# A two-layer hybrid transformer on one core: two-operand GpSimd work of the mixers on VectorE, the softmax's multiplication by 1/l on ScalarE

## The chip, the cores and the metric

The kernel runs on one core of a Trainium2 chip. A core has TensorE (PE: matmuls and transposes; PEld is its loading of stationary operands), VectorE (DVE), ScalarE (ACT), GpSimd (POOL) and SyncE (SP, which here issues DMAs). Each engine works through its own list of instructions in order; semaphores hold an instruction until what it needs is there. The metric is the device time of one execution in microseconds (us); the median of three runs is used.

## The reference

512 tokens of width 1024 pass two layers, each a mixer and a convolutional feed-forward part, all in float32.

```python
for i in range(DEPTH):                      # DEPTH = 2
    h = rmsnorm(x, mix_norms[i])
    x = x + (even_mixer(h, positions, *mixers[0]) if i % 2 == 0 else odd_mixer(h, *mixers[1]))
    x = x + conv_ffn(rmsnorm(x, ffn_norms[i]), *ffns[i])
return rmsnorm(x, final_norm)
```

The even mixer has two kinds of softmax attention. Twelve MLA heads attend causally over all keys; their queries and keys come from low-rank projections. Four heads (DSW) attend in three dilated windows at once, with rotary positions on query and key, and the three windows are merged by their sums. Both use `p = exp(s - max)`, `l = sum(p)`, `(p / l) @ v`.

The odd mixer has a state-space part (SSD) in 4 chunks of 128 tokens with 16 heads of 64, and 8 heads of stick-breaking attention:

```python
xdt = x * dt                                # SSD, per head and chunk
y_diag = (C B^T * decay) @ xdt
state = state * chunk_decay + B^T (xdt * decay_end)
y = y_diag + exp(cs) * (C @ state_before) + x * d_skip
log_w = log_sigmoid(z) + (sum of log_sigmoid(-z) over later keys)   # stick-breaking
y = exp(log_w) @ v
```

## The kernel before, in words

Activations lie transposed: 128 features on partitions, 512 tokens along the free dimension. To keep float32 accuracy, each operand of a matmul is split in a high part (a copy rounded to fp32r, mostly by ScalarE) and a low part (the rest, mostly by VectorE), and a product is three matmuls. So each tile that TensorE is to read costs ScalarE one pass and VectorE one pass. Weights come in chunks of up to 1024 columns by DMA (`wraw`), and `wchunk` (line 213) splits them: `whi` on ScalarE (line 219), `wlo` (line 221) on the engine named by `self.lo`: VectorE in the mixers, GpSimd in the two feed-forward parts. The change does not touch that.

Within a mixer, projections are cut in pieces of three to six matmuls and filled between the heads' own steps (`Stream.fill`); numbers written out by hand set how many. TensorE's order is fixed in that way (`InOrder`). For the other engines a scheduler sets the order of a queue when the program is built, from the dependences and its estimates.

Even mixer (line 644). `sincos` makes `cos` and `sin`; line 704 multiplies both by the token norms. For each of 12 query and key tiles of DSW, `run_qk` (line 719) evicts the projection twice: ScalarE writes `raw` (729), VectorE writes `rot = proj * cos` (730). Four DMAs of SP swap the 32-row quarters of `raw` into `sw` (733). Then `sw *= sin` (734) and `rot += sw` (735). `run_mla` makes the MLA operands: `vt` (759), `knp` (764), `rt` (773) and its split `qk` (264 and 265), and the key's halves `kh`, `kl` (871, 872).

`softmax` (line 572) works on one block of 128 queries, 64 times in all (16 heads of 4 blocks): VectorE adds the mask and takes the maximum (578), scales it (580); ScalarE takes the exponential and its sum `l` (581, two instructions: ACTIVATE and the read of the accumulator); VectorE takes the reciprocal (582); line 583 multiplies the block by it. Then TensorE transposes the probabilities, ScalarE and VectorE evict them as `pth` (600, 951) and `ptl` (601, 952), and TensorE multiplies with the values. While one head does this, the scores of the next are made. Two PSUM banks hold scores, two the transposes, two the results, two the projections.

Odd mixer, SSD (line 1118). `prepare` (1285) makes, for each half of the heads and each chunk, `xd = x * dt` (1292), its split `xdt` (1296, 1297), `xs *= d` (1300), `xd *= decay_end` (1302) and its split `xe` (264, 265). `states` (1307) makes the running state `stt`: the old one times the decay (1318), plus the new (1320), and its split `ph`. `past` (1323) adds the contribution of the state: `yof` (1332), `xs += yof` (1334). `weights` makes the decayed `C B^T` of a head (`sg`, 1348 and 1351) and its split `mh`; `apply` multiplies it with `xdt` and adds to `xs` (1366).

Stick-breaking attention (line 1441 on, heads from line 1497). A head has three banks. Each goes through ScalarE (1528 to 1530), VectorE (`ab`, 1531), a triangular select on GpSimd (1510), the split `sh` (a cast, 1535) and `sl` (1536), sums on TensorE, an exponential (1555), the select again, the split `wh` (a cast, 1559) and `wl` (1560), and the product with the values.

Of the kernel before, what the change touches and what calls it, by code (L numbers as in the profile page):

```python
# [10 lines left out]
F32 = mybir.dt.float32  # L11
# [3 lines left out]
AF = mybir.ActivationFunctionType  # L15
ALU = mybir.AluOpType
PSUM = bass.MemoryType.PSUM

P = 128
# [164 lines left out]
class Builder:  # L184
# [387 lines left out]
    def softmax(self, pool, s, n, tag, bufs, scale, mask):  # L572

        nc = self.nc
        st = pool.tile([P, 4], F32, tag="st", name=self.nm("st"), bufs=5)
        mx, nmx, l, rl = (st[:, k : k + 1] for k in range(4))
        t = pool.tile([P, n], F32, tag=tag, name=self.nm(tag), bufs=bufs)
        nc.vector.tensor_tensor_reduce(out=t, in0=s[:, :n], in1=mask, scale=1.0, scalar=-3.0e38,  # L578
                                       op0=ALU.add, op1=ALU.max, accum_out=mx)
        nc.vector.tensor_scalar(nmx, mx, -scale, None, op0=ALU.mult)  # L580
        nc.scalar.activation(t, t, AF.Exp, bias=nmx, scale=scale, accum_out=l)
        nc.vector.reciprocal(rl, l)  # L582
        nc.gpsimd.tensor_scalar(t, t, rl, None, op0=ALU.mult)  # L583
        return t

    def pv_steps(self, pool, o, blocks, v, first, last):
# [57 lines left out]
    def even_mixer(self, pool):  # L644
        nc, a = self.nc, self.a
# [55 lines left out]
        (qlh, qll), (klh, kll) = ([[t[k] for t in lh[c]] for k in range(2)] for c in (slice(0, 2), slice(2, 3)))  # L701

        for t in (cr, sr):
            nc.gpsimd.tensor_tensor(t, t, r, op=ALU.mult)

        masks = pool.tile([P, N_MASK], BF16, tag="masks", name="masks")
        for c0 in range(0, N_MASK, T):
# [11 lines left out]
        def run_qk(p, g, s):  # L719
            def run(w):  # L720
                for ps in self.proj_pieces(w, xh, xl):
                    yield
                raw = pool.tile([P, T], F32, tag="fr", name=self.nm("raw"), bufs=2)
                sw = pool.tile([P, T], F32, tag="fr", name=self.nm("sw"), bufs=2)
                t = pool.tile([P, T], F32, name=self.nm("rot"), tag="raw", bufs=8)
                view = k_order if s and g else q_order
                if s and not g:
                    view = lambda t, ordered=True: t
                nc.scalar.activation(raw, ps, AF.Copy)
                nc.vector.tensor_tensor(view(t), view(ps, False), view(cr, False), op=ALU.mult)  # L730
                for b in range(4):
                    o_ = b ^ 1
                    nc.sync.dma_start(sw[b * 32 : b * 32 + 32], raw[o_ * 32 : o_ * 32 + 32])
                nc.gpsimd.tensor_tensor(sw, sw, sr, op=ALU.mult)
                nc.gpsimd.tensor_tensor(view(t), view(t), view(sw, False), op=ALU.add)
                raws[p, g, s] = t

            return f"d{p}{g}{s}", lambda: self.wchunk(a["wqk0"][(p * 3 + g) * 2 + s], D), run
# [379 lines left out]
    def ssd(self, pool, sub, xh, xl, xs, ZS, zs, others):  # L1118
# [166 lines left out]
        def prepare(g):  # L1285

            xds = []
            for c in range(NB):
                x8 = xs[g][:, c].rearrange("p (h d) -> p h d", h=8)
                tq = lambda k: tok[:, k, c, g * 8 : g * 8 + 8, None].to_broadcast([P, 8, 64])  # L1290
                xd = sub.tile([P, 8, 64], F32, tag="xd", name=self.nm("xd"), bufs=2)
                (nc.vector if c % 2 else nc.gpsimd).tensor_tensor(xd, x8, tq(0), op=ALU.mult)
                for q in range(2):
                    h4 = slice(4 * q, 4 * q + 4)
                    sp = sub.tile([P, 4, 2, 64], F32R, name=self.nm("xdt"), **XD)
                    nc.scalar.activation(sp[:, :, 0, :], xd[:, h4], AF.Copy)
                    nc.vector.tensor_tensor(sp[:, :, 1, :], xd[:, h4], sp[:, :, 0, :].bitcast(F32), op=ALU.subtract)
                    xdt[g, c, q] = sp

                nc.gpsimd.tensor_tensor(x8, x8, dbc[:, g * 8 : g * 8 + 8, None].to_broadcast([P, 8, 64]), op=ALU.mult)  # L1300
                if c < NB - 1:
                    nc.gpsimd.tensor_tensor(xd, xd, tq(3), op=ALU.mult)
                    xde[g, c] = self.split(xd.rearrange("p h d -> p (h d)"), sub, "xe", bufs=6)

        state = {}
# [1 line left out]
        def states(g, c):  # L1307
# [6 lines left out]
            if c == 0:  # L1314
                nc.vector.tensor_copy(cur, ps)
            else:
                dec = cdec[:, c, g * 8 : g * 8 + 8, None].to_broadcast([P, 8, 64])
                nc.gpsimd.tensor_tensor(cur.rearrange("p (h d) -> p h d", h=8),
                                        state[g, c - 1][0].rearrange("p (h d) -> p h d", h=8), dec, op=ALU.mult)
                nc.vector.tensor_tensor(cur, ps, cur, op=ALU.add)  # L1320
            state[g, c] = cur, self.split(cur, sub, "ph", bufs=2)

        def past(g, c):
# [7 lines left out]
            tt = sub.tile([P, T], F32, tag="sg", name=self.nm("yof"), bufs=4)  # L1331
            nc.vector.tensor_tensor(tt.rearrange("p (h d) -> p h d", h=8),
                                    po.rearrange("p (h d) -> p h d", h=8), ec, op=ALU.mult)
            nc.gpsimd.tensor_tensor(xs[g][:, c], xs[g][:, c], tt, op=ALU.add)

        mix = {}

# [103 lines left out]
    def stick(self, pool, sub, zs, y, qkvs, others):  # L1441
# [55 lines left out]
        def head(h):  # L1497
# [41 lines left out]
            def sums(bi):  # L1539
# [17 lines left out]
                wh = sub.tile([P, T], F32R, tag="wh", name=self.nm("wh"), bufs=2)  # L1557
                wl = sub.tile([P, T], F32R, tag="wl", name=self.nm("wl"), bufs=2)
                nc.vector.tensor_copy(wh[:, :w], ab[:, :w])
                nc.gpsimd.tensor_tensor(wl[:, :w], ab[:, :w], wh[:, :w].bitcast(F32), op=ALU.subtract)  # L1560
                hd.w[bi] = wh, wl

            def apply(bi):
# [134 lines left out]
```

## Time and profile before

| | |
|---|---|
| median of 3 runs | 1465.1 us (1463.52 to 1468.44) |
| the profiled execution | 1463.86 us, its span 1462.1 us |
| instructions | 18180 |
| mean granted TensorE clock | 0.985 of full speed |
| DMA | 121.22 MB, mean 83 GB/s |

The span runs from the first to the last instruction. In the span, 0 to 338 us is the even mixer with its norms and first projections, 338 to 703 us the first feed-forward part, 703 to 1097 us the odd mixer (its SSD heads from about 772 to 910 us, its stick-breaking heads from about 910 to 1045 us), and the rest the second feed-forward part. Busy time is what an engine spent in instructions; a row that names a wait gives how long an engine stood idle before an instruction and what ended that. Granted clock is what a throttle gave TensorE; it is 1.00 or 0.50 at a time, and a mean over a stretch lies between.

### The profile page before, as it was taken

Reading aid. Unit: us, or ns where it says so; the run is one execution under the profiler, and the core shown is the slowest. Engines: PE = TensorE matmul, PEld = TensorE weight load, DVE = VectorE, ACT = ScalarE, POOL = GpSimd, SP = SyncE. Lnnn points to the kernel's source line nnn. Section 1 sums busy time; section 2 is a strip of 40 time slices with the busy share of each in tenths; the row PEclk is TensorE's granted clock in tenths of the full one; section 3 lists DMA queues with packets and bytes.
Section 4 is the critical chain, followed back from the end, with each engine's and each line's share of the span. In section 5 each row is a group of like instructions: output and inputs, shape, how many; then the busy total and the mean of one; then the engine's idle time right before and its main releaser. Section 6 shows DMA issues by size and latency. Waiting matters only on the chain.

```text
span 1462.1 us, 18180 instructions
## 1 busy us (share of the span) xinstructions
PE 1388.7 (95%) x6796; PEld 1146.8 (78%) x6796; DVE 863.6 (59%) x1362; ACT 663.2 (45%) x1085; POOL 597.1 (41%) x391
## 2 busy tenths in 40 slices
PE   7899899899999999999988898998999999999997
PEld 5777687687888888888877677787888888888886
DVE  7878678746555555122668987678555555552124
ACT  5557457535433333222446465777344333333222
POOL 2454445303655555444102420434215555554441
PEclk9999999999999999999999999999999999999998
DMA  4421212122322322333222111111233233223333
GB/s 166 120 62 55 69 55 69 39 81 73 101 93 95 101 101 85 105 92 95 92 72 73 44 44 58 46 58 40 62 101 101 87 102 101 91 97 94 100 98 98
DMA packets 40264, 121.22 MB, mean 83 GB/s; under 512 B 5232, under 2 KB 8304, under 8 KB 40176
## 3 DMA queue, kind: packets, MB, share of 16 engines
q1 hardware_dynamic: 38160, 117.92, 25.4%
q10 hardware_dynamic: 2016, 2.14, 0.5%
q8 instruction: 54, 0.88, 0.3%
q14 instruction: 34, 0.28, 0.1%
HBM read 114.80 MB, written 2.10 MB: 80 GB/s over the span
## 4 chain that ended last, share of the span: by engine, by line
PE 80%; DVE 12%; ACT 4%; issue 3%; POOL 1%; DMA 1%; DVEq 0%; SPq 0%; ACTq 0%; POOLq 0%
PE proj L113 50%; PE o L113 19%; PE z L113 5%; PE s L113 3%; PE t L116 2%; DVE wlo L221 2%; PE t L113 1%; ACT whi L219 1%; DVE mh L265 1%; DVE sg L1351 0%; DVE cv L1150 0%; DVE xs L1366 0%; DVE xl L331 0%; DVE s L578 0%; DVE rot L730 0%
## 5 line engine op out<-in xcount | busy, mean ns | idle before, releaser
L221 POOL TENSOR_TENSOR wlo<-wraw,whi 128x1024 fp32r<-128x1024 f32 (+1 forms) x135 | 315.2, 2336 | 323.7 <-ACT whi L219 323.7
L219 ACT ACTIVATE whi<-wraw 128x1024 fp32r<-128x1024 f32 (+3 forms) x219 | 222.2, 1015 | 365.0 <-PE proj L113 328.7
L113 PE MATMUL proj<-xh,whi 128*128 128x512 f32 x844 | 343.0, 406 | 8.8 <-ACT xh L330 6.7
L113 PE MATMUL proj<-xh,wlo 128*128 128x512 f32 x844 | 334.1, 396 | 1.4 <-DVE wlo L387 1.1
L113 PE MATMUL proj<-xl,whi 128*128 128x512 f32 x844 | 333.9, 396 | 1.2 <-DVE xl L331 1.2
L113 PE MATMUL proj<-act,whi 128*128 128x512 f32 (+1 forms) x748 | 219.3, 377 | 0.0
L113 PEld LDWEIGHTS proj<-xh,whi 128*128 128x128 f32 x844 | 161.3, 191 | 41.0 <-ACT xh L330 8.7
L113 PEld LDWEIGHTS proj<-xh,wlo 128*128 128x128 f32 x844 | 160.9, 191 | 37.6 <-DVE wlo L387 1.5
L113 PEld LDWEIGHTS proj<-xl,whi 128*128 128x128 f32 x844 | 161.2, 191 | 31.3 <-DVE xl L331 3.1
L113 PEld LDWEIGHTS proj<-act,whi 128*128 128x128 f32 x748 | 137.7, 188 | 25.8
L113 PE MATMUL o<-xh,wlo 128*128 128x512 f32 x368 | 143.4, 390 | 0.0
L113 PE MATMUL o<-xh,whi 128*128 128x512 f32 x368 | 143.3, 389 | 0.0
L113 PE MATMUL o<-xl,whi 128*128 128x512 f32 x368 | 143.2, 389 | 0.0
L113 PE MATMUL proj<-act,wlo 128*128 128x512 f32 (+1 forms) x374 | 140.8, 376 | 0.0
L583 POOL TENSOR_SCALAR s<-s,st 128x512 f32<-128x512 f32 (+1 forms) x64 | 81.2, 1274 | 109.4 <-DVE st L582 82.3
L366 DVE TENSOR_TENSOR x<-x,proj 128x512 f32<-128x512 f32 x31 | 21.2, 684 | 171.0 <-PE proj L113 170.9
L221 DVE TENSOR_TENSOR wlo<-wraw,whi 128x1024 fp32r<-128x1024 f32 (+3 forms) x84 | 100.0, 1190 | 27.3 <-ACT whi L219 26.3
L524 DVE SCALAR_TENSOR_TENSOR cv<-gt,cols,cv 128x511 f32<-128x511 f32 x44 | 94.3, 2148 | 35.9 <-ACT cv L523 35.9
L528 POOL TENSOR_TENSOR sl<-sl,rsr 128x512 f32<-128x512 f32 x44 | 57.8, 1313 | 94.3 <-ACT sl L527 94.3
L527 ACT ACTIVATE sl<-cv 128x512 f32<-128x512 f32 x44 | 27.8, 631 | 127.3 <-DVE cv L525 127.3
L533 DVE TENSOR_TENSOR up<-sl,o 128x512 f32<-128x512 f32 x44 | 30.3, 688 | 91.8 <-POOL sl L528 91.8
L265 DVE TENSOR_TENSOR act<-up,act 128x512 fp32r<-128x512 f32 x44 | 63.3, 1438 | 29.3 <-ACT act L264 29.3
(305 smaller groups left out, 2250.9 us busy)
## 6 DMA issues: line engine op xcount, KB each, us to landing
wraw<-in_g SPq DMA_DIRECT2D x44, 512.0 KB, 3.3
wraw<-in_u SPq DMA_DIRECT2D x44, 512.0 KB, 3.3
wraw<-in_d SPq DMA_DIRECT2D x32, 448.0 KB, 3.3
wraw<-in_wqk SPq DMA_DIRECT2D x20, 512.0 KB, 3.5
wraw<-in_d SPq DMA_DIRECT2D x17, 512.0 KB, 3.5
wraw<-in_wx SPq DMA_DIRECT2D x12, 512.0 KB, 3.4
wraw<-in_wv SPq DMA_DIRECT2D x10, 512.0 KB, 3.6
wraw<-in_wz SPq DMA_DIRECT2D x8, 512.0 KB, 3.3
```

The source lines that it names most:

```text
L113: return self._put(self.b.nc.tensor.matmul(*args, **kw))
L116: return self._put(self.b.nc.tensor.transpose(*args))
L219: nc.scalar.activation(hi[:, :n], raw[:, :n], AF.Copy)
L221: (eng or self.lo).tensor_tensor(lo[:, :n], raw[:, :n], hi[:, :n].bitcast(F32), op=ALU.subtract)
L265: nc.vector.tensor_tensor(lo, src, hi.bitcast(F32), op=ALU.subtract)
L366: self.nc.vector.tensor_tensor(self.x[m], self.x[m], ps, op=ALU.add)
L524: nc.vector.scalar_tensor_tensor(c[:, 1:], gt[:, : T - 1], col_(1), c[:, 1:], op0=ALU.mult, op1=ALU.add)
L527: nc.scalar.activation(s, c, AF.Silu)
L528: nc.gpsimd.tensor_tensor(s, s, r, op=ALU.mult)
L533: nc.vector.tensor_tensor(u, s, pu, op=ALU.mult)
L583: nc.gpsimd.tensor_scalar(t, t, rl, None, op0=ALU.mult)
```

## The change

Lines keep their numbers. Line 583, the multiplication of a probability block by 1/l, becomes a copy with a per-partition scale on ScalarE. Lines 704, 734, 735, 1292 (its half that was on GpSimd), 1300, 1302, 1318, 1334 and 1560 go from GpSimd to VectorE with the same operands. GpSimd keeps the selects of line 1510, the conversions of the masks, four squares at the start (654), and its work in the feed-forward parts and the end.

```diff
@@ softmax
         nc.vector.reciprocal(rl, l)
-        nc.gpsimd.tensor_scalar(t, t, rl, None, op0=ALU.mult)
+        nc.scalar.activation(t, t, AF.Copy, scale=rl)
@@ even_mixer
         for t in (cr, sr):
-            nc.gpsimd.tensor_tensor(t, t, r, op=ALU.mult)
+            nc.vector.tensor_tensor(t, t, r, op=ALU.mult)
...
-                nc.gpsimd.tensor_tensor(sw, sw, sr, op=ALU.mult)
-                nc.gpsimd.tensor_tensor(view(t), view(t), view(sw, False), op=ALU.add)
+                nc.vector.tensor_tensor(sw, sw, sr, op=ALU.mult)
+                nc.vector.tensor_tensor(view(t), view(t), view(sw, False), op=ALU.add)
@@ ssd, prepare
-                (nc.vector if c % 2 else nc.gpsimd).tensor_tensor(xd, x8, tq(0), op=ALU.mult)
+                nc.vector.tensor_tensor(xd, x8, tq(0), op=ALU.mult)
...
-                nc.gpsimd.tensor_tensor(x8, x8, dbc[:, g * 8 : g * 8 + 8, None].to_broadcast([P, 8, 64]), op=ALU.mult)
+                nc.vector.tensor_tensor(x8, x8, dbc[:, g * 8 : g * 8 + 8, None].to_broadcast([P, 8, 64]), op=ALU.mult)
                 if c < NB - 1:
-                    nc.gpsimd.tensor_tensor(xd, xd, tq(3), op=ALU.mult)
+                    nc.vector.tensor_tensor(xd, xd, tq(3), op=ALU.mult)
@@ ssd, states and past
-                nc.gpsimd.tensor_tensor(cur.rearrange("p (h d) -> p h d", h=8),
+                nc.vector.tensor_tensor(cur.rearrange("p (h d) -> p h d", h=8),
...
-            nc.gpsimd.tensor_tensor(xs[g][:, c], xs[g][:, c], tt, op=ALU.add)
+            nc.vector.tensor_tensor(xs[g][:, c], xs[g][:, c], tt, op=ALU.add)
@@ stick, sums
-                nc.gpsimd.tensor_tensor(wl[:, :w], ab[:, :w], wh[:, :w].bitcast(F32), op=ALU.subtract)
+                nc.vector.tensor_tensor(wl[:, :w], ab[:, :w], wh[:, :w].bitcast(F32), op=ALU.subtract)
```

The order of TensorE's and SP's instructions stays as it was. VectorE's and ScalarE's queues change at many places; three follow. Tiles carry the program's names with a number for the buffer.

ScalarE at the first softmax of the even mixer (in the profile before at 69 to 78 us), first before:

```order
L581 ACT_TABLE_LOAD
L581 ACTIVATE s_127_657,st_656<-s_127_657,st_656 128x512
L581 ACTIVATE s_130_671,st_670<-s_130_671,st_670 128x384
L581 ACTIVATE s_133_685,st_684<-s_133_685,st_684 128x256
L581 ACTIVATE s_136_699,st_698<-s_136_699,st_698 128x128
L219 ACTIVATE whi_746<-wraw_744 128x1024
```

The same place of ScalarE's queue now:

```order
L581 ACT_TABLE_LOAD
L581 ACTIVATE s_127_657,st_656<-s_127_657,st_656 128x512
L583 ACTIVATE s_127_657<-s_127_657,st_656 128x512
L581 ACTIVATE s_130_671,st_670<-s_130_671,st_670 128x384
L583 ACTIVATE s_130_671<-s_130_671,st_670 128x384
L581 ACTIVATE s_133_685,st_684<-s_133_685,st_684 128x256
L583 ACTIVATE s_133_685<-s_133_685,st_684 128x256
L581 ACTIVATE s_136_699,st_698<-s_136_699,st_698 128x128
L583 ACTIVATE s_136_699<-s_136_699,st_698 128x128
L219 ACTIVATE whi_746<-wraw_744 128x1024
```

The multiplication of a block stands right behind its exponential, ahead of the next block's exponential and of the next weight chunk.

VectorE at the same first MLA head (in the profile before at 64 to 71 us), first before:

```order
L773 TENSOR_TENSOR rt_612<-proj_605,qt_521 128x512
L872 TENSOR_TENSOR kl_569<-knp_603,kh_568 64x512
L872 TENSOR_TENSOR kl_573<-knp_603,kh_572 64x512
L629 TENSOR_TENSOR v_623<-t_618,v_623 128x8x64
L773 TENSOR_TENSOR rt_633<-proj_626,qt_525 128x512
L265 TENSOR_TENSOR qk_615<-rt_612,qk_614 128x512
L221 TENSOR_TENSOR wlo_646<-wraw_642,whi_644 128x768
L265 TENSOR_TENSOR qk_636<-rt_633,qk_635 128x512
```

The same place of VectorE's queue now:

```order
L734 TENSOR_TENSOR sw_577<-sw_577,sin 128x512
L773 TENSOR_TENSOR rt_612<-proj_605,qt_521 128x512
L872 TENSOR_TENSOR kl_569<-knp_603,kh_568 64x512
L872 TENSOR_TENSOR kl_573<-knp_603,kh_572 64x512
L735 TENSOR_TENSOR rot_578<-rot_578,sw_577 128x512
L629 TENSOR_TENSOR v_623<-t_618,v_623 128x8x64
L773 TENSOR_TENSOR rt_633<-proj_626,qt_525 128x512
L221 TENSOR_TENSOR wlo_646<-wraw_642,whi_644 128x768
L265 TENSOR_TENSOR qk_615<-rt_612,qk_614 128x512
L265 TENSOR_TENSOR qk_636<-rt_633,qk_635 128x512
```

Lines 734 and 735 came in between, and the weights' low part `wlo_646` stands ahead of the query's low part `qk_615`, where it stood behind.

VectorE in the stick-breaking part at the start of a pair of heads (in the profile before at 956 to 962 us), first before:

```order
L1531 SCALAR_TENSOR_TENSOR ab_8206<-z_8203,ab_8206 128x512
L1559 CAST wh_8268<-ab_8126 128x384
L265 TENSOR_TENSOR yd_8248<-yp_8034,yd_8247 128x512
L1078 TENSOR_TENSOR gt_8308<-proj_8236,rsr_6053 128x512
L1535 CAST sh_8212<-ab_8206 128x512
L221 TENSOR_TENSOR wlo_8320<-wraw_8316,whi_8318 128x1024
L1559 CAST wh_8304<-ab_8185 128x384
L1536 TENSOR_TENSOR sl_8213<-ab_8206,sh_8212 128x512
```

The same place of VectorE's queue now:

```order
L1531 SCALAR_TENSOR_TENSOR ab_8206<-z_8203,ab_8206 128x512
L1535 CAST sh_8212<-ab_8206 128x512
L265 TENSOR_TENSOR yd_8248<-yp_8034,yd_8247 128x512
L1559 CAST wh_8268<-ab_8126 128x384
L1078 TENSOR_TENSOR gt_8308<-proj_8236,rsr_6053 128x512
L1536 TENSOR_TENSOR sl_8213<-ab_8206,sh_8212 128x512
L221 TENSOR_TENSOR wlo_8320<-wraw_8316,whi_8318 128x1024
L1560 TENSOR_TENSOR wl_8269<-ab_8126,wh_8268 128x384
L1559 CAST wh_8304<-ab_8185 128x384
```

`sl_8213` moved ahead of the weight chunk and of a cast, `sh_8212` ahead of three others, and `wl_8269` came in behind the weight chunk.

## The prediction

> **What bounds the kernel now.** I read the page first, then the busy time by stage, then the list of what TensorE waited for, then the timeline at the waits that touch the change.
>
> The page's head, TensorE's row and the chain by engine:
>
> ```profile
> span 1462.1 us, 18180 instructions
> PE 1388.7 (95%) x6796; PEld 1146.8 (78%) x6796; DVE 863.6 (59%) x1362; ACT 663.2 (45%) x1085; POOL 597.1 (41%) x391
> PE 80%; DVE 12%; ACT 4%; issue 3%; POOL 1%; DMA 1%; DVEq 0%; SPq 0%; ACTq 0%; POOLq 0%
> ```
>
> TensorE is busy 95% and carries 80% of the chain; GpSimd (POOL) carries 1%. Its 41% busy is work beside the path, so emptying it gains nothing by itself. 73 us of the span have no matmul; that is all the change can work on, plus the half-speed clock that follows some gaps.
>
> Busy time by stage, start to end, then PE, PEld, DVE, ACT, POOL, and the granted clock. 56 to 310 is the attention of the first layer, 338 to 703 a feed-forward stage, 772 to 910 the SSD part, 910 to 1045 the stick-breaking attention:
>
> ```profile
> 56.00:150.00 94.00, 84.10 (x466) 68.23 (x466) 76.35 (x187) 57.02 (x123) 45.24 (x35) 0.98 0.23 68
> 200.00:310.00 110.00, 101.49 (x650) 83.56 (x650) 83.34 (x205) 63.91 (x137) 46.22 (x35) 1.00 0.19 55
> 338.00:703.00 365.00, 364.36 (x1614) 301.82 (x1614) 161.10 (x154) 124.71 (x155) 186.14 (x90) 1.00 0.30 96
> 772.00:910.00 138.00, 122.47 (x619) 98.49 (x617) 120.06 (x192) 80.21 (x166) 37.31 (x28) 0.96 0.16 54
> 910.00:1045.00 135.00, 126.16 (x624) 105.31 (x625) 99.08 (x162) 91.66 (x160) 54.56 (x73) 0.97 0.16 49
> ```
>
> The feed-forward stage leaves TensorE idle for under 1 us of 365, and the change does not touch it. In the mixers TensorE misses 8 to 16 us a stretch, with VectorE 73 to 87% busy: waits are short and mostly for VectorE. The list of TensorE's waits says so (total us, times, longest):
>
> ```profile
> PE o L113 <- DVE xdt L1297: 6.4, 2, 3.9
> PE o L113 <- DVE ptl L601: 5.1, 4, 1.8
> PE proj L113 <- DVE vt L759: 4.5, 4, 1.4
> PE z L113 <- DVE sl L1536: 4.4, 3, 1.6
> PE s L113 <- DVE qk L265: 2.4, 1, 2.4
> PE t L116 <- POOL s L583: 2.1, 3, 1.1
> PE o L113 <- POOL wl L1560: 0.6, 1, 0.6
> ```
>
> Only the last two name the instructions that move: 2.7 us. So the change works through queues: less latency from GpSimd, more work on VectorE and ScalarE (ACT), and what GpSimd no longer does to VectorE.
>
> **What one operation costs.** The same multiplication on both engines (line 1292), then two VectorE groups of the SSD stretch (ns least, median, most; then busy us and mean ns):
>
> ```profile
> L1292 POOL TENSOR_TENSOR xd<-xs,tok x4: 1042/1404/1427, 772.3 to 831.8; 128x512 f32<-128x512 f32 x4
> L1292 DVE TENSOR_TENSOR xd<-xs,tok x4: 693/1526/1532, 772.7 to 833.7; 128x512 f32<-128x512 f32 x4
> L265 DVE TENSOR_TENSOR mh<-sg,mh x16: 672/682/1530, 797.9 to 893.4; 128x512 fp32r<-128x512 f32 x16
> L265 DVE TENSOR_TENSOR mh<-sg,mh 128x512 fp32r<-128x512 f32 x16 | 13.3, 834 | 0.9 <-ACT mh L264 0.9
> L1297 DVE TENSOR_TENSOR xdt<-xd,xdt x16: 408/422/1271, 774.2 to 849.3; 128x256 fp32r<-128x256 f32 x16
> L1297 DVE TENSOR_TENSOR xdt<-xd,xdt 128x256 fp32r<-128x256 f32 x16 | 10.7, 711 | 0.5 <-ACT xdt L1296 0.5
> ```
>
> VectorE needs 0.69 us where GpSimd needs 1.04 to 1.43. But VectorE's own operations with two operands in SBUF have two durations, 0.67 and about 1.5 us. Over their least, the mh group lost 13.3 - 16 x 0.67 = 2.6 us, xdt 10.7 - 16 x 0.41 = 4.2, and the line 1292 group on VectorE, median 1.53 of four, about 2.5: together 9 us lost to something that in the timeline always stands beside a two-operand GpSimd instruction. The Trainium skill, "SBUF — State Buffer", section "SBUF: two separate sides", has the mechanism: such a VectorE operation and a GpSimd instruction lock a shared port pair for a whole instruction, the loser blocks. These rows agree.
>
> **SSD part.** 4 + 8 + 6 + 4 + 6 = 28 instructions (lines 1292, 1300, 1302, 1318, 1334) move to VectorE: 28 x 0.69 = 19.3 us at most, 17 where they stand back to back. Removed: 9 us in the three groups above, and I put 15 us on the stretch, since the other two-operand groups there (ph, xe, sg) sit in the same queue. So VectorE's sum rises by some 3 us and each link from a GpSimd result gets 0.4 to 0.7 us shorter. VectorE has 138 - 120 = 18 us idle there. I take 0; bounds: -4 (the two xdt waits halve, with some clock) to +8 (19.3 less 11, if 11 is all that was lost and nothing hides it).
>
> **First layer.** Lines 704, 734 and 735 move 26 instructions to VectorE, and line 583 moves 64 to ScalarE. Rows for the prices:
>
> ```profile
> L730 DVE TENSOR_TENSOR rot<-proj,cos x12: 684/1046/1079, 44.3 to 228.9; 128x512 f32<-128x512 f32 x12
> POOL sw L734 <- DMA sw<-raw: 20.8, 5, 5.9
> L440 ACT ACTIVATE x<-x,cols 128x512 f32<-128x512 f32 x7 | 5.1, 725 | 0.2
> L581 ACT ACTIVATE s<-s,st 128x384 f32<-128x384 f32 x16 | 9.8, 610 | 8.7 <-DVE st L580 8.5
> L581 ACT ACTIVATE s<-s,st 128x256 f32<-128x256 f32 x12 | 6.1, 506 | 9.4 <-DVE st L580 9.4
> L581 ACT ACTIVATE s<-s,st 128x128 f32<-128x128 f32 x12 | 4.8, 398 | 2.8 <-DVE st L580 1.3 <-POOL s L583 1.3
> L556 DVE TENSOR_SCALAR angk<-ang 128x512 f32<-128x512 f32 x2 | 0.8, 418 | 0.0
> L583 POOL TENSOR_SCALAR s<-s,st 128x512 f32<-128x512 f32 (+1 forms) x64 | 81.2, 1274 | 109.4 <-DVE st L582 82.3 <-DVE st L580 15.9 <-PE t L116 11.2
> ```
>
> The copy with a scale from a column (line 440) is the new operation: 24 x 0.725 + 16 x 0.61 + 12 x 0.506 + 12 x 0.398 = 38 us on ScalarE, for 81 us off GpSimd. ScalarE rises from 61% (57 of 94, 64 of 110) to about 75%. VectorE gets 14 x 0.69 + 12 x 1.05 (strided like line 730; bounds 0.69 to 1.63 by GpSimd's own) = 22 us, less the collisions that go; no row groups those, and I set 0.3 us for each of the 26, 8 us.
>
> The Trainium skill, "ScalarE: Activation LUTs", section "Rules for kernel authors", speaks against this choice: multiplications belong on VectorE. The trace agrees for a multiplication by a column, 0.42 us on VectorE (line 556) against 0.725; by that rule the 64 would cost at most 64 x 0.42 = 27 us on VectorE and nothing on ScalarE. The sum would lose the +3.6 set for ScalarE's queue below and owe a like amount to VectorE's.
>
> A wait moves too: line 734 waited 20.8 us on GpSimd for the swapping DMAs, and behind it on VectorE now stand the mask step, the low parts and the evictions. The new order sets four to eight instructions between line 730 and line 734, about the 2 to 3 us that matter after line 730's end, so I take 0 (bounds 0 and 12 x 0.5 = 6).
>
> The worst place is the first softmax. VectorE and ScalarE there, before:
>
> ```profile
> 71.49 0.56 DVE L578 CUSTOM_DVE_ANT_0 s<-s,masks 128x384 f32<-128x384 f32 x1
> 72.16 0.72 ACT L581 ACTIVATE s<-s,st 128x512 f32<-128x512 f32 x1 [1.50 <-DVE st L580]
> 72.78 0.19 ACT L581 ACTIVATION_READ_ACCUMULATOR s<-s,st 128x1 f32 x1
> 77.29 1.06 ACT L219 ACTIVATE whi<-wraw 128x1024 fp32r<-128x1024 f32 x1 [1.60 <-issue]
> 79.52 1.05 DVE L730 TENSOR_TENSOR rot<-proj,cos 128x512 f32<-128x512 f32 x1
> 80.62 0.50 PE L113 MATMUL proj<-lh,whi 128*128 128x512 f32 x1 [1.47 <-DVE rot L730]
> ```
>
> Now exponential and multiplication alternate on ScalarE, and each reciprocal stands on VectorE ahead of the next mask step, so the two engines take turns: 0.72 + 0.19 + 0.2 + 0.73 for the first block, then mask and exponential of the next. Four blocks end near 78.4, and whi starts 1.1 us later than 77.29; vt now stands ahead of rot on VectorE, 0.6 more. TensorE waits 1.7 us longer: +1.7. In the other 15 heads the multiplications are spread between evictions. Each head brings 2.2 to 2.8 us to ScalarE's queue, ahead of pth, kh and whi; bounds 0 and one operation a head on the path, 15 x 0.72 = 10.8. I take a third of one, +3.6, since 25% of ScalarE stays idle. The waits for GpSimd's s go: -2.1, of which 0.6 comes back as ScalarE's own time: -1.5. At 69 us the low part wlo now stands ahead of qk, for which TensorE waits: +0.5. Sum +4.3.
>
> **Stick-breaking part.** 24 instructions (line 1560) move: 16 x 0.56 + 8 x 0.69 = 14.5 us on VectorE, of 36 us idle (0.56 is line 1536's usual time, below). The order helps at one place:
>
> ```profile
> L1536 DVE TENSOR_TENSOR sl<-ab,sh x24: 545/559/1560, 922.9 to 1034.3; 128x384 fp32r<-128x384 f32 x16, 128x512 fp32r<-128x512 f32 x8
> 958.89 1.30 DVE L221 TENSOR_TENSOR wlo<-wraw,whi 128x1024 fp32r<-128x1024 f32 x1
> 960.39 0.68 DVE L1536 TENSOR_TENSOR sl<-ab,sh 128x512 fp32r<-128x512 f32 x1
> 961.12 0.63 PE L113 MATMUL z<-sl,trir 128*128 128x512 f32 x1 [1.59 <-DVE sl L1536]
> 961.33:964.74 3.41, 3.41 (x14) 3.31 (x14) 2.83 (x5) 0.75 (x2) 1.25 (x3) 0.50 0.41 143
> ```
>
> TensorE waits here for sl, which stands behind wlo and a cast; the new order sets sl ahead of both: about -1.4, and the same again one pair of heads later. After the gap the clock is 0.50 for 3.41 us, worth 1.7 us; with the shorter gap I take it as gone once. Against that, VectorE's extra work delays other things by about 0.8. Sum -3.7; bounds -7 and +3.
>
> **Sum.** 0 + 4.3 - 3.7 = +0.6 on the profiled execution's 1463.86 us (span 1462.1 and 1.8 around it): 1464.4. The median of the runs is 1465.1, 1.2 above, so 1465.5. About 0.3%, or 4.4 us, is what a measurement of this kernel can tell from no change; I forecast no change.
>
> **Rivals.** (A) Slower: ScalarE's queue. If a multiplication stands in front of an eviction in every head, the 15 heads cost 10.8 instead of 3.6: +7.8 in all, 1473. It decides once waits of TensorE for ptl, pth, vt and rot in 56 to 310, with 5.1 + 4.5 us in two rows above, grow by more than 8 us. For it: ScalarE is strictly in order here and the multiplication must wait for VectorE's reciprocal. Against: GpSimd's 1.27 us mean per step was slower than what replaces it, and 2.1 us is all that TensorE waited for it. (B) Faster: the collisions are the path. SSD gives -4, stick -7 with two clock windows, and the first layer only +1, since VectorE also loses its 1.5 us operations there: -10, 1455. For it: TensorE's largest waits (xdt 6.4, sl 4.4) are for operations that run double. Against: VectorE takes over nearly as much work as it gets back. It is what the Trainium skill, "SBUF — State Buffer", section "SBUF: two separate sides", would make of the time. (C) Nothing: GpSimd is off the path and all hides; it falls inside the forecast.
>
> **Numbers.** Forecast 0.40 (1461 to 1470), A 0.30 (1470 to 1477), B 0.30 (1451 to 1461). Leaving a tenth out on each side, the range is 1454 to 1475; the forecast's own is 1461 to 1470. The forecast's edges add 0.01 to either sign and take 0.02 from it: faster 0.31, same 0.38, slower 0.31.
>
> **What would show it.** Right: VectorE's mh and xdt groups of the SSD part at 0.68 and 0.42 us mean; line 583 on ScalarE at 0.7 us for 512 columns; TensorE's wait for sl down to about 1.5 us; more waits between 70 and 300 us. Wrong: the SSD stretch shorter by more than 4 us, the first layer changed by more than 8 us either way, or VectorE groups still at 1.5 us beside a GpSimd that hardly works.

## The result and the profile after

The change made the kernel faster: 1459.13 us (median of 6 runs, 1456.82 to 1460.37) against 1466.91 (6 runs), ratio 0.9947, 95% interval 0.9930 to 0.9964. Eleven more runs of it beside its parts gave 0.9964 (0.9952 to 0.9976). So it gains 5 to 8 us; the forecast was no change.

The page's head, TensorE's row and the chain by engine after the change:

```profile
span 1457.4 us, 17947 instructions
PE 1385.9 (95%) x6796; PEld 1142.6 (78%) x6796; DVE 879.9 (60%) x1440; ACT 694.5 (48%) x1149; POOL 411.9 (28%) x249
PE 78%; DVE 13%; ACT 5%; issue 2%; DMA 1%; POOL 0%; SPq 0%; DVEq 0%; ACTq 0%; POOLq 0%
```

GpSimd lost 185 us of work and VectorE gained only 16, as its doubled instructions are gone. Busy time by stage, columns as before the change:

```profile
56.00:150.00 94.00, 81.67 (x418) 65.30 (x417) 76.66 (x192) 66.30 (x144) 0.00 (x0) 0.98 0.22 64
200.00:310.00 110.00, 102.07 (x640) 83.65 (x638) 86.63 (x216) 79.52 (x168) 0.00 (x0) 0.98 0.19 58
772.00:910.00 138.00, 124.27 (x634) 101.09 (x633) 121.01 (x222) 81.60 (x167) 0.00 (x0) 0.98 0.16 55
910.00:1045.00 135.00, 128.97 (x653) 106.97 (x652) 107.20 (x188) 92.96 (x163) 26.03 (x49) 1.00 0.16 49
```

In the SSD stretch VectorE does 30 instructions more in 121 us, where it had 120. The last column but two is the granted clock: 0.98 for 0.96 in the SSD part, 1.00 for 0.97 in the stick-breaking part, but 0.98 for 1.00 from 200 to 310 us. What TensorE waited for (total us, times, longest):

```profile
PE proj L113 <- DVE vt L759: 5.3, 5, 1.3
PE o L113 <- DVE xdt L1297: 5.3, 2, 3.2
PE o L113 <- DVE mh L265: 4.0, 3, 2.0
PE t L116 <- ACT s L583: 3.7, 5, 1.4
PE o L113 <- DVE ptl L601: 2.6, 3, 1.3
PE z L113 <- DVE sl L1536: 2.4, 4, 1.2
PE o L113 <- DVE wl L1560: 1.7, 4, 1.0
```

Some waits shrank (ptl 5.1 to 2.6, sl 4.4 to 2.4), others grew (vt 4.5 to 5.3, s 2.1 to 3.7, wl 0.6 to 1.7; the longest for mh 1.2 to 2.0). Added up over all gaps between its matmuls from 40 to 1100 us, TensorE waits 54.5 us before and 52.3 after: 2 us less, which doesn't explain the gain. Their lengths changed more: 14 gaps over 1.4 us before (8 up to 341 us, 3 from 700 to 910 us, 3 in the stick-breaking part), 8 after (4, 4 and none).

The two VectorE groups of the SSD part (busy us and mean ns at the end), then, from the view of one line, line 583 on ScalarE (ns least, median, most):

```profile
L265 DVE TENSOR_TENSOR mh<-sg,mh 128x512 fp32r<-128x512 f32 x16 | 10.9, 680 | 0.0
L1297 DVE TENSOR_TENSOR xdt<-xd,xdt 128x256 fp32r<-128x256 f32 x16 | 6.2, 414 | 0.0
```

```profile
L583 ACT ACTIVATE s<-s,st x64: 385/606/727, 74.0 to 304.5; 128x512 f32<-128x512 f32 x24, 128x384 f32<-128x384 f32 x16, 128x256 f32<-128x256 f32 x12, 128x128 f32<-128x128 f32 x12
```

The two groups are at 0.68 and 0.41 us, and line 583 takes 0.73 us at most: the durations are those forecast. At the first softmax ScalarE alternates as the new order says, with VectorE in between; the timeline of its engine, then of TensorE 7 us on:

```profile
72.97 0.72 ACT L581 ACTIVATE s<-s,st 128x512 f32<-128x512 f32 x1 [1.06 <-DVE st L580]
74.02 0.73 ACT L583 ACTIVATE s<-s,st 128x512 f32<-128x512 f32 x1 [0.23 <-DVE st L582]
75.08 0.62 ACT L581 ACTIVATE s<-s,st 128x384 f32<-128x384 f32 x1 [0.34 <-DVE st L580]
...
82.38 0.50 PE L113 MATMUL proj<-lh,whi 128*128 128x512 f32 x1 [1.06 <-DVE vt L759]
```

TensorE waits 1.06 us there, for vt, where it waited 1.47 for rot: the 1.7 us more that the forecast set here did not come.

### The profile page after: what moved, and what is told of

It reads as the page before. It is cut to its first block, busy times and chain, and to the rows that moved or that the text cites. A ratio compares the mean times of both kernels' runs of the same rounds, so it can differ in the third digit from the quotient of the medians.

```text
span 1457.4 us, 17947 instructions
## 1 busy us (share of the span) xinstructions
PE 1385.9 (95%) x6796; PEld 1142.6 (78%) x6796; DVE 879.9 (60%) x1440; ACT 694.5 (48%) x1149; POOL 411.9 (28%) x249
## 4 chain that ended last, share of the span: by engine, by line
PE 78%; DVE 13%; ACT 5%; issue 2%; DMA 1%; POOL 0%; SPq 0%; DVEq 0%; ACTq 0%; POOLq 0%
PE proj L113 49%; PE o L113 19%; PE z L113 5%; PE s L113 2%; DVE wlo L221 2%; PE t L116 2%; PE t L113 1%; ACT whi L219 1%; ACT s L583 1%; DMA sw<-raw 1%; DVE xl L331 0%; DVE cv L1150 0%; DVE mh L265 0%; DMA x<-in_x 0%; DVE x L366 0%
## 5 line engine op out<-in xcount | busy, mean ns | idle before, releaser
L221 DVE TENSOR_TENSOR wlo<-wraw,whi 128x1024 fp32r<-128x1024 f32 (+3 forms) x84 | 95.6, 1138 | 28.9 <-ACT whi L219 27.9
L113 PEld LDWEIGHTS o<-xh,wlo 128*128 128x128 f32 x368 | 69.1, 188 | 14.4
```

The source lines that it names most:

```text
L113: return self._put(self.b.nc.tensor.matmul(*args, **kw))
L221: (eng or self.lo).tensor_tensor(lo[:, :n], raw[:, :n], hi[:, :n].bitcast(F32), op=ALU.subtract)
```

## The experiments

Each run of a kernel has a span and a mean granted clock. Span times (1 - clock) is half the time spent at half clock; I call it the loss, and span times clock the rest. Half clock during a wait costs nothing, so the loss is an upper bound of what half clock costs; where it matters, the profile's own account stands beside it (TensorE's work at full clock plus its waits, from its first matmul to its last). Means over all runs; the ratio is to the kernel before on the same chip; the last column counts TensorE's waits over 1.4 us from 40 to 1100 us in the one profile.

| kernel | runs | ratio (95%) | clock | span x clock | loss | waits > 1.4 |
|---|---|---|---|---|---|---|
| before | 66 | 1 | 0.9835 | 1439.8 | 24.1 | 14 |
| the change | 17 | 0.9947 and 0.9964 | 0.9894 | 1442.0 | 15.4 | 8 |
| e1 softmax only | 12 | 1.0006 (0.9993 to 1.0018) | 0.9833 | 1440.1 | 24.4 | 10 |
| e2 odd mixer only | 12 | 0.9954 (0.9937 to 0.9971) | 0.9857 | 1436.0 | 20.9 | 12 |
| e3 rope only | 6 | 1.0063 (1.0040 to 1.0085) | 0.9823 | 1446.6 | 26.0 | 14 |
| e4 one-tile GpSimd | 6 | 0.9931 (0.9909 to 0.9953) | 0.9855 | 1432.4 | 21.1 | 9 |
| e5 first layer only | 6 | 1.0054 (1.0036 to 1.0071) | 0.9830 | 1445.6 | 25.0 | 11 |
| e6 all but rope | 7 | 0.9948 (0.9930 to 0.9967) | 0.9870 | 1437.0 | 18.9 | 8 |
| e7 line 583 on VectorE | 6 | 1.0041 (1.0025 to 1.0057) | 0.9838 | 1445.5 | 23.8 | 16 |
| e9 before, idle matmuls | 6 | 0.9953 (0.9940 to 0.9966) | 0.9910 | 1444.9 | 13.1 | 8 |
| e10 change, idle matmuls | 6 | 0.9957 (0.9942 to 0.9971) | 0.9895 | 1443.4 | 15.3 | 5 |
| e11 e6, idle matmuls | 6 | 0.9927 (0.9912 to 0.9943) | 0.9898 | 1439.4 | 14.8 | 5 |
| e12 SSD only | 12 | 0.9982 (0.9969 to 0.9994) | 0.9828 | 1437.2 | 25.1 | 15 |
| e13 e10, two more | 5 | 0.9956 (0.9943 to 0.9970) | 0.9918 | 1444.8 | 11.9 | 5 |
| e14 rope, multiplications | 5 | 1.0060 (1.0047 to 1.0073) | 0.9798 | 1442.2 | 29.7 | 14 |
| e15 rope, addition | 5 | 1.0051 (1.0039 to 1.0064) | 0.9804 | 1441.8 | 28.8 | 16 |
| e16 e11, two more | 5 | 0.9928 (0.9916 to 0.9941) | 0.9918 | 1440.7 | 11.9 | 3 |

The products (span times clock) agree within 0.5 us between the means of the four lots of the kernel before (1439.5 to 1440.0), though its times spread from 1460 to 1471 us: most of that spread goes with the clock. Run by run its product lies between 1437.5 and 1442.6 us.

### The parts alone (e1, e2, e3)

Each takes some lines of the change's diff and leaves the rest as before. e1:

```diff
-        nc.gpsimd.tensor_scalar(t, t, rl, None, op0=ALU.mult)
+        nc.scalar.activation(t, t, AF.Copy, scale=rl)
```

> Only line 583 goes to ScalarE; all the rest stays on GpSimd as before. Theory S (ScalarE's queue is what made the first layer 7 us longer in the trace after): time +4 to +8 us against before, TensorE waits for line 583's s and for ptl and vt, ScalarE 37 us busier. Theory R (the 26 rope instructions on VectorE made it longer): within 1.5 us of before. The record's sum: +3.8 (+1.7 in the first softmax, +3.6 in the other heads, -1.5 for GpSimd's s).

Measured +0.6 us by medians, product 1440.1: nothing. Theory S fell, and so did the record's +3.8. ScalarE had room: it is 71 and 72% busy in the first two stretches above.

e2 takes the lines of the odd mixer, for example:

```diff
-            nc.gpsimd.tensor_tensor(xs[g][:, c], xs[g][:, c], tt, op=ALU.add)
+            nc.vector.tensor_tensor(xs[g][:, c], xs[g][:, c], tt, op=ALU.add)
```

> Only the odd mixer's 52 instructions go to VectorE (lines 1292, 1300, 1302, 1318, 1334, 1560); the first layer stays as before. Theory C (VectorE's doubled two-operand instructions were on the path): -8 to -12 us against before, the trace's odd mixer 8 to 10 us shorter, mh at 0.68 and xdt at 0.41 us. The record's sum: -3.7 us, all of it in the stick-breaking part. If the gain after the change came only from half-clock windows that fall differently from run to run: between -4 and 0.

Measured -5.7 us by medians, a little under theory C's -8; product -3.8, loss -3.2. By the profiles' account it is -5.8.

e3 takes lines 704, 734 and 735:

```diff
-                nc.gpsimd.tensor_tensor(sw, sw, sr, op=ALU.mult)
+                nc.vector.tensor_tensor(sw, sw, sr, op=ALU.mult)
```

> Only lines 704, 734 and 735 go to VectorE. Theory S (line 583 is what lengthened the first layer): between -3 and +1 us, since VectorE's operations beside GpSimd's also get shorter there. Theory R (VectorE waiting for the swapping DMAs, or its extra 22 us, lengthened the first layer): +4 to +8 us. The record's sum: +0.5.

Measured +9.3 us, product +6.8 (by the profiles' account +4.6): theory R. What VectorE waited for at line 734 in e3, and below it what TensorE waited for from 56 to 310 us:

```profile
DVE sw L734 <- DMA sw<-raw: 3.0, 4, 1.2
```

```profile
PE proj L113 <- DVE vt L759: 6.7, 5, 2.5
PE t L116 <- POOL s L583: 5.3, 6, 2.0
PE s L113 <- DVE qk L265: 3.1, 2, 2.1
```

VectorE stood only 3.0 us behind the DMAs. The price is its fuller queue: vt 4.5 to 6.7, qk 2.4 to 3.1, and s 2.1 to 5.3 although line 583 did not move. The steps ahead of it are VectorE's: GpSimd's idle time until VectorE's reciprocal (line 582) grew from 82.3 to 131.4 us.

### Why the odd mixer gained (e4, e12)

e4 leaves the work on GpSimd, but with one tile and a column as operands, so that the odd mixer's values are others:

```diff
-                nc.gpsimd.tensor_tensor(x8, x8, dbc[:, g * 8 : g * 8 + 8, None].to_broadcast([P, 8, 64]), op=ALU.mult)
+                nc.gpsimd.tensor_scalar(xs[g][:, c], xs[g][:, c], dbc[:, g * 8 : g * 8 + 1], None, op0=ALU.mult)
...
-            nc.gpsimd.tensor_tensor(xs[g][:, c], xs[g][:, c], tt, op=ALU.add)
+            nc.gpsimd.tensor_scalar(xs[g][:, c], tt, tok[:, 2, c, g * 8 : g * 8 + 1], None, op0=ALU.mult)
...
-                nc.gpsimd.tensor_tensor(wl[:, :w], ab[:, :w], wh[:, :w].bitcast(F32), op=ALU.subtract)
+                nc.gpsimd.tensor_scalar(wl[:, :w], wh[:, :w].bitcast(F32), self.cols[:, 0:1], None, op0=ALU.mult)
```

> GpSimd keeps its 52 instructions of the odd mixer, but each in a form with one tile and a column in place of two tiles (line 1292's GpSimd half, 1300, 1302, 1318, 1334, 1560), so the values of that part are not the reference's. Theory C (two-tile GpSimd instructions double VectorE's two-tile ones, and that is the path): mh at 0.68 to 0.75, xdt at 0.41 to 0.45 us mean, and -5 to -12 us against before although GpSimd does as many instructions as before. Theory L (the gain comes from GpSimd's slower instructions and its detour being gone from the chain): within 2 us of before, whatever VectorE's durations. If GpSimd's one-tile form holds VectorE up as well: mh stays at 0.8 and the time at 0.

Measured -9.8 us by medians, product -7.4, with GpSimd doing as many instructions as before. A GpSimd group of e4 in the SSD stretch (its second line has ns least, median, most) and the same two VectorE groups, then TensorE's wait for xdt there:

```profile
L1300 POOL TENSOR_SCALAR xs<-xs,hb 128x512 f32<-128x512 f32 x8 | 14.2, 1788 | 1.3 <-DVE xd L1292 1.2
L1300 POOL TENSOR_SCALAR xs<-xs,hb x8: 1562/1646/2477, 776.8 to 833.1; 128x512 f32<-128x512 f32 x8
L265 DVE TENSOR_TENSOR mh<-sg,mh 128x512 fp32r<-128x512 f32 x16 | 11.6, 723 | 0.2
L1297 DVE TENSOR_TENSOR xdt<-xd,xdt 128x256 fp32r<-128x256 f32 x16 | 7.3, 496 | 0.0
```

```profile
PE o L113 <- DVE xdt L1297: 1.7, 2, 1.0
```

Before, line 1300 on GpSimd took 1202 ns, from this row:

```profile
L1300 POOL TENSOR_TENSOR xs<-xs,hb 128x512 f32<-128x512 f32 x8 | 9.6, 1202 | 2.9 <-DVE xd L1292 2.6
```

With one tile as operand GpSimd's instruction became longer (1202 to 1788 ns) and VectorE's nearly the short one (mh 834 to 723, xdt 711 to 496, a little over the 0.45 us of the expectation), and TensorE's wait for xdt fell from 6.4 to 1.7 us. Most of the 1788 ns is the form's own length: line 583 takes 1565 ns for 512 columns in the profile before where no VectorE instruction runs beside it. So theory C holds: it was the collision of two-tile instructions, not GpSimd's slowness, that cost the odd mixer. The Trainium skill, "SBUF — State Buffer", section "SBUF: two separate sides", lets any GpSimd instruction that reads SBUF block a two-input VectorE one; here one-tile GpSimd instructions read SBUF too and hardly blocked it (over the whole of e4, the 512-column subtractions of line 265 take 684 ns with neither kind of GpSimd instruction beside them, 743 beside one-tile ones, 1448 beside two-tile ones), so on that point the measurement decides.

e12 takes the SSD part's lines alone.

> Only the SSD part's 28 instructions (lines 1292, 1300, 1302, 1318, 1334) go to VectorE. The record's term for SSD: 0 (-4 to +8), and -3.7 for the stick-breaking part. By span times clock the whole odd mixer gave 1440.0 to 1436.0, -4: if the record's split is right, span times clock stays at 1440 +- 1 here and the time within 2 us of before; if SSD carries it (theory C, VectorE's doubled instructions), span times clock is 1436 to 1438 and the time -3 to -6 us.

Measured -2.3 us by medians, product -2.6, loss +1.0 (noise). So SSD gives 2.6 of the odd mixer's 3.8 (by the profiles' account 3.0 of 5.8), which the record had at 0; the time misses theory C's -3 to -6. The loss falls only when the stick-breaking part moves too (e2: 20.9).

### Interaction and placement (e5 to e8)

e5 is e1 and e3 together, e6 the whole change without lines 704, 734 and 735, e8 the change unaltered; e7 is the change with

```diff
-        nc.scalar.activation(t, t, AF.Copy, scale=rl)
+        nc.vector.tensor_scalar(t, t, rl, None, op0=ALU.mult)
```

> Both edits of the first layer, lines 583, 704, 734 and 735; the odd mixer stays as before. Theory A (the parts add): line 583 alone measured +0.6 us, rope alone +9.3, so +8 to +11 against before. Theory I (rope on VectorE costs only while line 583 is on GpSimd, where TensorE waited 5.3 us for s in the rope run): -1 to +3. The trace after had its first layer 5.7 to 7.2 us longer. The record's sum: +4.3.

> The whole change but the rope lines 704, 734 and 735, which stay on GpSimd. Theory A (the parts add): +0.6 - 6.7 = -6 us against before, and as the parts with rope would give +3, the whole change's -7.8 would have to come from somewhere else, such as fewer half-clock windows. Theory I (rope costs nothing beside line 583 on ScalarE): -7 to -9, the same as the whole change. If rope costs its 9 us in the whole change too: -14 to -17.

> The whole change, but line 583 as a multiplication by a column on VectorE in place of ScalarE. By the 0.42 us of line 556 for 512 columns it adds at most 27 us to VectorE and takes 38 us off ScalarE. If ScalarE's queue is what lengthens the first layer: 3 to 6 us faster than the whole change. If VectorE's queue is what TensorE waits for there (theory V, from the rope run): 3 to 10 us slower than the whole change.

> The whole change once more, unaltered, for more runs on the same chip as its parts and a second profile. If the half-clock windows fall by chance: again -5 to -10 us against before in the median, but another number of windows than 7 plus the one at the end, and a profiled time that differs from its median by up to 4 us. If the number of windows belongs to the kernel: 6 to 8 windows again.

e5 measured +7.7 us by medians and e2 -5.7, which would make +2.0; the change is -5 to -8. In the products the parts do add: +5.8 for e5, -3.8 for e2, sum +2.0, and the change has +2.2. By the profiles' own account it is 1433.7 before, 1433.4 in both profiles of the change: -0.3, where e5 has +4.4 and e2 -5.8. So without the clock the change is worth between nothing and +2 us, and its gain is the loss, 24.1 to 15.4. In the profiles 71% of the loss before and 75% of it after fell on TensorE's work and not on its waits (15.5 of 21.7 us, 11.5 of 15.3); by these shares of the mean losses I estimate the clock's part of the gain at about 5.5 us. e8's profile has 11 half-clock stretches ahead of the end where the first one of the change had 7 (before: 10), and its profiled execution was the slowest of its eleven (1464.64): the count varies from run to run, only its mean belongs to the kernel.

e6 measured -7.6 us by its ratio, the time that theory I gave, but not for its reason: in the products rope costs 5.0 us in the change as well (1442.0 less 1437.0; by the profiles' account 3.9), and leaving it out gained little because the loss is larger (18.9 for 15.4). e7 is 6.4 us slower than before and 12 slower than the change; there TensorE waits 6.4 us for s:

```profile
PE t L116 <- DVE s L583: 6.4, 4, 2.7
```

So VectorE's queue is the one that is waited for in the first layer (theory V). The Trainium skill's rule to put multiplications on VectorE ("ScalarE: Activation LUTs", section "Rules for kernel authors"), which the prediction weighed, would have lost the whole gain here.

### The clock (e9, e10, e11, e13, e16)

The granted clock is 1.00 or 0.50 in stretches of 3.413 us on a fixed grid. I cut the 14 profiles up to e12 along that grid and counted, from 60 us on, how often a stretch at full clock was followed by one at half, by TensorE's idle time in it:

| idle in a stretch, us | up to 1.0 | 1.0-1.2 | 1.2-1.4 | 1.4-1.6 | 1.6-1.8 | 1.8-2.0 | over 2.0 |
|---|---|---|---|---|---|---|---|
| followed by half clock | 4 of 5236 | 7 of 97 | 13 of 59 | 15 of 59 | 8 of 14 | 11 of 12 | 48 of 48 |

A wait of 1 us costs 1 us; one of 2 us inside a stretch costs up to 1.7 more. The table is a count, which moves by two or three cases with where the grid is set, and it has no sharp border: the share rises from 22% at 1.2-1.4 us to all cases over 2.0. The 1.4 us of the last column above is chosen from it; e1 with 10 such waits and a loss of 24.4 shows that it is a guide and no formula. e9 tests the cause. It puts matmuls of the identity, which nobody reads, ahead of six of the longer waits of the kernel before:

```diff
+    def idle_fill(self, out, n):
+        i, k = self.ident, out.shape[1] // P
+        for _ in range(n):
+            self.pe.matmul(out.rearrange("p (a b) -> p a b", a=k), i, i[:, None, :].to_broadcast([P, k, P]),
+                           start=True, stop=True, skip_group_check=True)
...
                 ps = self.psum("s")
+                self.idle_fill(ps, FILL[1])
                 sums, all_ = (ps[:, k * 64 : k * 64 + 64].rearrange("p (c h) -> p c h", c=NB) for k in range(2))
```

> The kernel before, with matmuls of the identity, whose results nobody reads, put into TensorE's queue where it waited longest in the trace before: 2 of 512 columns ahead of the first scores (wait 2.4 us for qk), 3 ahead of the sums of dt (3.9 us for sp), 6 of 256 and 8 of 128 columns inside the first SSD head (3.9 and 2.5 us for xdt), and one of 512 at two stick-breaking heads (1.6 us for sl). No other instruction changes. Theory K (a stretch of 3.41 us in which TensorE idles more than about 1.4 us is followed by one at half clock, and the change gained by having fewer of those): the mean granted clock rises from 0.984 to 0.988 to 0.991, -5 to -9 us against before, span times clock as before within 1.5 us. Theory L (the gain is shorter waits; the clock falls as it likes): clock 0.984, time 0 to +3 us.

Measured 1459.43 us against 1466.55, with clock 0.9910: theory K on clock and time, though the product rose by 5.1, more than the 1.5 expected. By the profiles' account the kernel is 2.4 us longer, as some idle matmuls outlast the wait; the rest of the 5.1 is no longer work, but comes from waits at half clock, which the product counts half (6.2 us of loss stood in waits in the profile before, 3.5 in e9's). Three filled places before (start and end, then PE, PEld, DVE, ACT, POOL, clock):

```profile
738.00:752.00 14.00, 10.14 (x44) 8.52 (x43) 10.04 (x26) 5.59 (x10) 0.00 (x0) 0.76 0.18 56
798.00:816.00 18.00, 11.59 (x49) 8.95 (x48) 17.02 (x21) 6.25 (x14) 10.81 (x9) 0.81 0.16 56
956.00:968.00 12.00, 9.71 (x42) 8.13 (x41) 9.84 (x17) 7.75 (x15) 6.18 (x9) 0.86 0.14 44
```

The same in e9:

```profile
738.00:752.00 14.00, 12.72 (x63) 9.59 (x62) 10.47 (x26) 7.28 (x13) 0.00 (x0) 1.00 0.23 75
798.00:816.00 18.00, 16.07 (x89) 12.99 (x88) 17.48 (x25) 7.13 (x17) 12.15 (x9) 1.00 0.08 30
956.00:968.00 12.00, 10.56 (x50) 8.07 (x49) 9.63 (x17) 8.11 (x16) 5.37 (x7) 1.00 0.14 44
```

The other engines have the same instructions as before, and the clock stays at 1.00 in all three; elsewhere e9's profile keeps 6 half-clock stretches. TensorE did 12 us more work (1385.6 us at full clock for 1373.2), and the kernel got faster by as much as the change gained. The Trainium skill, "TensorE: Matmul & The Clock Gate", section "What's actually happening", has a free-running window of 3413 ns, which these traces show; its section "HAM oscillation — how this bites in real kernels" warns of idle gaps over about 3.4 us. Here over 2 us of idle time in a stretch was always enough, and 1.2 to 1.6 us in 28 of 118 stretches, so the measurement decides.

e10 adds the same to the change (but for the stick-breaking part's), e11 to e6.

> The whole change with the same idle matmuls, but for the two of the stick-breaking part, whose waits were 0.5 us there already. Theory K: the clock rises from 0.9895 to 0.992 or more, -4 to -7 us against the whole change, -10 to -13 against before. Theory L: 0 to +3 us against the whole change.

> Line 583 and the odd mixer's lines changed, rope left on GpSimd, with the idle matmuls. Without them it measured -7.6 us against before at clock 0.987, span times clock 1437. Theory K: clock 0.991 or more, -12 to -16 us against before, the fastest of all that are correct. Theory L: -5 to -8.

e10 missed: no gain over the change, loss 15.3. In its profile no half clock is left at the filled places, but three stretches came at 843, 860 and 897 us. The wait at 842 us is 2.01 us in both. The change's timeline, and the stretch around it:

```profile
843.70 1.00 PE L113 MATMUL o<-xdt,mh 128*128 128x128 f32 x7 [2.01 <-DVE mh L265]
```

```profile
838.00:848.00 10.00, 7.99 (x39) 6.03 (x38) 10.00 (x21) 4.96 (x12) 0.00 (x0) 1.00 0.14 53
```

That was the change; here is e10 (its lines stand nine further down), its timeline and the stretch around it:

```profile
842.23 1.29 PE L113 MATMUL o<-xdt,mh 128*128 128x128 f32 x7 [2.01 <-DVE mh L274]
```

```profile
838.00:848.00 10.00, 7.99 (x32) 6.04 (x31) 9.02 (x18) 4.97 (x12) 0.00 (x0) 0.83 0.13 50
```

Same wait, same work of TensorE, other place on the grid: in the change's profile the border cut it so that 1.51 us fell into one stretch, in e10 2.01 did. e11 measured 1456.0 us, 0.9927: the fastest kernel that computes the reference's result, but it is 10.6 us faster than before where 12 to 16 were expected, at clock 0.9898 for 0.991.

e13 and e16 add two matmuls for that wait to e10 and e11. They stand inside one head's sum and change that head's result.

```diff
+                if hh == 6 and c == 0:
+                    self.idle_fill(py[:, P:], 2)
```

> The whole change with the idle matmuls of the run before, and 2 more of 384 columns in the seventh SSD head, where TensorE waited 2.0 us for the low part of mh and where the half-clock stretches at 843, 860 and 897 us began. Theory K (idle stretches over about 1.4 us set the clock): these three go, the mean clock rises from 0.9895 to 0.992 to 0.994, -3 to -5 us against the change with fewer idle matmuls. Theory L: the clock stays at 0.9895, time 0 to +1.

> Line 583 and the odd mixer changed, rope on GpSimd, all idle matmuls and the 2 more in the seventh SSD head (2.0 us of wait there too). Theory K: clock from 0.990 to 0.992 or more, 1452 to 1455 us, the fastest. Theory L: 1456 to 1457.

The clock rose to 0.9918 in both, with no half clock left from 362 to 1440 us in their profiles: theory K on the clock. It missed on time: the ratios stayed (0.9956 for 0.9957, 0.9928 for 0.9927), and e16's 1454.5 us lies in its range only because the kernel before ran faster on that chip (1464.6 for 1466.6). The product rose by 1.3 us as the loss fell by 3, and the rest is within the intervals. So in the change too TensorE's waits set the clock, but filling them never made the change itself faster: the idle matmuls cost about what the clock gave back.

### Rope's two halves (e14, e15)

e14 moves lines 704 and 734, e15 line 735.

> Of the first layer only lines 704 and 734 (the multiplications by cos, sin) go to VectorE. Rope as a whole measured 1446.6 against 1440.0 us of span times clock, +6.7. Theory D (VectorE stands behind the swapping DMAs at line 734, and the evictions behind it are late): +5 to +7 of span times clock here, +1 or less for line 735 alone. Theory V (VectorE is full there, and each instruction costs by its length, 0.69 against 1.07 us): +2 to +3.5.

> Of the first layer only line 735 (the strided addition) goes to VectorE. Theory V: +3 to +5 us of span times clock. Theory D: -1 to +1.

Products +2.4 and +2.0 us (standard error 0.8 each): theory V for e14, theory D rejected, e15 a little under V's +3. Together they cost 6.8, which may be more than the sum; by the profiles' account they are +1.9 and +2.8, and +4.6 together, so there they add. In time each alone costs as much as both, +9.0 and +8.3, since the loss rises to 29.7 and 28.8. Why half a rope leaves the clock worse than a whole one is not settled; the counts of waits over 1.4 us (14 and 16) only fit it roughly.

## Why the prediction was wrong

- **The sum without the clock came out near by luck.** The record had 0 + 4.3 - 3.7, of which -1.7 was one half-clock stretch: +2.3 without it. Measured: product +2.2, by the profiles -0.3. Its parts were wrong and cancelled. (Its last line should read 1465.1 + 0.6 = 1465.7, not 1465.5, which changes nothing.)
- **First layer:** +4.3 forecast, +5.8 measured (e5; by the profiles' account +4.4), but the terms were swapped. "Worst place" (+1.7) and "a third of one" multiplication a head on ScalarE (+3.6): e1 shows +0.3 in all. Rope was put at no more than its DMA wait, 0 (bounds 0 to 6): e3 shows +6.8, of which only 3.0 us of VectorE's time stood behind DMAs. This term failed too: it counted the 22 us on VectorE as hidden, with VectorE 81% busy from 56 to 150 us; the qk term (+0.5) was the part of it that was seen.
- **SSD:** 0 forecast, -2.6 measured (by the profiles' account -3.0), inside its bounds. VectorE's sum rose by 1 us where 3 were forecast.
- **Stick-breaking:** waits -2.0 forecast, -1.2 measured by product and -2.8 by the profiles' account (e2 less e12); the order helped where the record said (sl 4.4 to 2.4 us, no wait over 1.2, though 1.5 us in all was forecast).
- **The clock is the step that failed.** The record took it "as gone once", -1.7 us; the loss fell by 8.7. It was priced at one place, and the sum was otherwise made of waits as though each microsecond weighed the same. By the table, shrinking an idle time of 1.6 to 2 us in a stretch to 1.0 to 1.4 removes most of the half-clock stretches behind it, and adding waits of 0.5 us costs little but themselves. The change did that in the stick-breaking part: 3 waits over 1.4 us became none, two for sl by its new place and one for gt (line 1078, 2.0 to 0.7). In the first layer the waits over 1.4 us fell from 8 to 4 (e1 has 4 there too), but the half-clock stretches up to 365 us did not: 3 before, 4 and 5 in the change's two profiles. From 700 to 1060 us the six profiles with the odd mixer as before have 7 or 8 stretches, the five with it moved and nothing filled 3 to 7, on average 2.1 fewer, some 3.6 us of loss. No part alone has the loss of the whole, 15.4: where the rest of the 8.7 comes from, and how the parts' losses combine, stays open.
- **Rival B** had the sign, its collisions are shown (e4), and it counted two clock windows where the forecast had one. But it put the odd mixer at -11 us, where e2 measured -5.7, and the first layer at +1, where e5's product and profile gave +5.8 and +4.4. Rival A is refuted by e1.

## What to carry to other kernels

Where the granted clock is below 1 anywhere, sort the waits of TensorE by length before pricing them: here one that falls from 1.6 to 1.1 us can be worth up to 2 us, one that grows from 0.2 to 0.7 costs 0.5. Compare kernels by span times clock and by the loss apart, over many runs, since one profile's count of half-clock stretches is a draw. And ask of each engine that takes over work how full it is in that stretch, not in the whole kernel: ScalarE took 64 multiplications for nothing, VectorE 26 others for 5 to 7 us.

## What the runs showed that was not expected

Extra matmuls that compute nothing made the kernel before 7 us faster. A multiplication of one tile by a column takes GpSimd longer than one of two tiles (1562 for 1042 ns at the least), yet it hardly holds VectorE's two-tile instructions up (mh 723 ns, 834 beside the shorter ones). The kernel before runs from 1460 to 1471 us with its span times clock constant to about 0.5 us in the mean.
